# State-space and convolution stage on one core: operations grouped, elementwise work moved from GpSimd to VectorE

## The chip, the cores and the metric

One core of a Trainium2 chip runs one inference step of a hybrid decoder layer as a single program. The metric is the device time of one execution in microseconds (us). Five engines work side by side: TensorE (PE; its weight loads are listed as PEld), VectorE (DVE), ScalarE (ACT), GpSimd (POOL) and SyncE (SP), which here issues the transfers.

## The reference, cut to what matters

A prompt of 1024 tokens and 8 samples of 4 tokens go through the same layer. First comes the mixer, which the change touches: a convolution group and a state-space group side by side. Then follow cross-attention into 256 memory tokens and a SwiGLU network, each with a norm before and after.

```python
def token_mixer(h, conv_buf, ssm_h0, ...):
    z = h @ w_in
    a, g, u = z[..., :512], z[..., 512:1024], z[..., 1024:]
    v = a * jax.nn.sigmoid(g)
    v_ext = jnp.concatenate([conv_buf, v], axis=1)
    c = jax.nn.silu(layer_norm(causal_depthwise_conv(v_ext, w_dw, b_dw), ln_g, ln_b))
    s, h_last = s5_layer(u, ssm_h0, ...)
    return jnp.concatenate([c, s], axis=-1) @ w_out, conv_new, h_last

def s5_layer(u, h0, ...):              # 32 groups of 16 channels, 64 complex states each
    a_bar = jnp.exp(lam * dt)
    b_bar = ((a_bar - 1.0) / lam)[:, :, None] * b_mat
    bu = jnp.einsum("btgp,gnp->btgn", uf, b_bar)
    bu = bu.at[:, 0].add(a_bar * h0)
    _, hs = lax.associative_scan(_ssm_combine, (a_seq, bu), axis=1)
    y = jnp.einsum("btgn,gpn->btgp", hs, c_mat).real + d_skip * uf
    y = jax.nn.gelu(y)
    return y * jax.nn.sigmoid(y @ w_glu), hs[:, -1]
```

## The kernel before, in words

Activations lie with channels on the 128 partitions. The 1056 tokens are two blocks b of 2 x 264 columns: 8 sample columns and 256 prompt columns in each half. Matrix products use each operand as a high and a low part, three products each.

The program opens with `tokens_in`, which turns the token rows over on TensorE into tiles tagged `xf` (13 buffers, line 289), and with small tables for the state space: `turns`, `pw` (powers of a_bar), `pwr` (the same reversed), `rho`, `cmat` and `bbar`. Then `run(filler(), s5_stream())` (line 822) interleaves two streams, and this is the stage that the change touches.

`s5_stream` goes through 16 pairs of channel groups; two pairs make a super group `sg`. Four time steps are folded into one column, so each pair scans 256 columns. `s5_matrices` (line 682) builds the block matrices `ebd` (from `bbar` and `pwr`, four steps) and `fbd` (from `cmat` and `pw`, five steps): complex products, written as two real products into `ct0` and `ct1` and a sum or difference per output part `o` and per half `g` of the partitions. `s5_matrices2` transposes `ebd` (psS), multiplies it with `fbd` (psK, with the skip term `dd`) and copies both out. `s5_table` (line 669) makes cosine and sine of the turn of each column for one pair: the sum of a coarse and a fine turn and the subtraction of the rounded turn on GpSimd, the rounding on VectorE, absolute value and two sines on ScalarE, into a table `tab` of two buffers. `s5_states` (line 735) multiplies the inputs on TensorE into a PSUM tile, copies the sample columns out on ScalarE (`wsam`), turns the rest back (X and Y on VectorE, their sums on GpSimd), scans real and imaginary part with `tensor_tensor_scan` (M, VectorE), turns forward again (X on VectorE, Y on GpSimd) and writes `hx` (VectorE); GpSimd writes the start values into `hx` and the final state into `hfin`. `s5_outputs` (line 766) makes the outputs of the pair two behind on TensorE and ScalarE's gelu. X, Y and M have two buffers each, `hx` three. psS, psK and the output tile `py` share two PSUM tiles.

`filler` carries the convolution group in four blocks `ct` of 128 channels. `conv_input` (line 560) projects gate and value, with the sigmoid on ScalarE and the gate's second multiplication (`sg`, line 577) on GpSimd. `conv` (line 622) makes the prompt's convolution as products with small banded matrices `cm`, built in turn by VectorE and GpSimd in two buffers (line 639), five products into `pcv` each. `conv_samples` (line 610) convolves the samples' columns: for each of 8 samples a product with the taps on GpSimd into `sp` (one buffer) and two reductions on VectorE, put behind all else by a low priority. `conv_tail` packs the new convolution state (`pk`) on GpSimd.

The order on each engine is fixed when the program is built: a scheduler places instructions by priority (order in the source, moved by `high_priority`) against a simulated time line, and a tile is handed out when a buffer of its tag is free. On the chip each engine works through its own list in order and waits by semaphores.

Of the kernel before, what the change touches and what calls it, by code (L numbers as in the profile page):

```python
# [8 lines left out]
F32 = mybir.dt.float32  # L9
# [3 lines left out]
AF = mybir.ActivationFunctionType  # L13
# [5 lines left out]
P = 128  # L19
# [23 lines left out]
def decode_step(ctx: ExitStack, tc: tile.TileContext, I, O):  # L43
# [36 lines left out]
    def tt(out, a, b, op, eng=None):  # L80
        (eng or dve).tensor_tensor(out, a, b, op)  # L81
# [198 lines left out]
    def tokens_in(b):  # L280
        for k in range(KT):
            c = slice(k * P, (k + 1) * P)
            pt = mm_tile(f"xt{b}{k}")
            for s in range(2):
                q = slice(32 * (2 * b + s), 32 * (2 * b + s) + 8)
                for i in range(2):
                    pe.transpose(pt[:, s, 8 + i * P:8 + (i + 1) * P], rows[b][s][i][:, c], ident)
                pe.transpose(pt[:, s, 0:8], srows[q, c], ident[q, q])
            xt = startp.tile([P, 2, W], F32, tag="xf", bufs=13, name=f"xf{b}{k}")
            act.activation(xt, pt[:, :, :W], AF.Copy)  # L290
            sync.dma_start(xres[b][k], xt)
# [219 lines left out]
    pe.transpose(ph[:, 128:256], h0row[:, 1, :], ident)  # L511
    h0 = sp5.tile([P, 2, NB, 16], F32, tag="h0", name="h0")
    dve.tensor_copy(h0, ph[:, 0:256].rearrange("p (i b a) -> p i b a", i=2, b=NB))
    cmat = sp5.tile([P, 2, 16, 16], F32, tag="cmat", name="cmat")
    for i, sign in enumerate((1.0, -1.0)):
        pc = sm_tile(f"pc{i}")
        for j in range(4):
            pe.transpose(pc[:, j * P:(j + 1) * P], crow[i][:, j, :], ident)
        pcv = pc.rearrange("p (a g q) -> p a g q", g=2, q=16)
        for g in range(2):  # L520
            q = slice(64 * g, 64 * g + 64)
            act.activation(cmat[q, i], pcv[q, :, g, :], AF.Copy, scale=sign)

    bbar = sp5.tile([P, 2, 16, 16], F32, tag="bbar", name="bbar")
    b1 = unit("b1", F32, (P, 16, 16), "co")

    def bc(x, n):
        return x.unsqueeze(2).to_broadcast([P, x.shape[1], n])

    for o, (x, y, op) in enumerate(((f_re, f_im, ALU.subtract), (f_im, f_re, ALU.add))):  # L530
        tt(bbar[:, o], bc(x, 16), bmat[:, 0], ALU.mult, pool)
        tt(b1, bc(y, 16), bmat[:, 1], ALU.mult, pool)
        tt(bbar[:, o], bbar[:, o], b1, op, pool)

    run(gt[1])
    with tc.high_priority(offset=1000000):
# [23 lines left out]
    def conv_input(ct):  # L560
# [10 lines left out]
        for b in range(2):  # L571
            pg = mm_tile(f"pg{ct}{b}")
            dense(pg, wgh, wgl, h[b])
            sg = tmp(f"sg{ct}{b}")
            tt(sg, pg[:, :, :W], r0[b], ALU.mult)
            act.activation(sg, sg, AF.Sigmoid)
            tt(sg, sg, r0[b], ALU.mult, pool)
            yield
            pa = mm_tile(f"pa{ct}{b}")
            dense(pa, wah, wal, h[b])  # L580
            tt(view(vt, 2 * b * CH + 4, [(CH, 2), (4 * CH, 2), (1, P)]), view(pa, 8, [(512, 2), (1, 2), (2, P)]),
               view(sg, 8, [(W, 2), (1, 2), (2, P)]), ALU.mult)
# [6 lines left out]
    def conv_tail(ct):  # L589
# [7 lines left out]
                           pst[:, 128 * i:128 * i + 120].rearrange("p (b r) -> p b r", r=30), AF.Copy)  # L597
        background(conv_samples, ct)
        pk = mx.tile([P, 64], F32, tag="pk", name=f"pk{ct}")
        pool.tensor_copy(pk[:, 0:32].rearrange("p (s b) -> p s b", s=4), vs[:, :, 30:34].rearrange("p b s -> p s b"))  # L600
        pool.tensor_copy(pk[:, 32:64].rearrange("p (j s) -> p s j", s=8), vt[:, :, CH - 4:])
        pr = mm_tile(f"pcr{ct}")[:, 0]
        pe.transpose(pr[:64, 0:P], pk, ident)
        cr = mx.tile([64, P], F32, tag="cr", name=f"cr{ct}")
# [5 lines left out]
    def conv_samples(ct):  # L610
        vs = vss[ct]
        w = taps[:, ct]
        for i in range(8):
            sp = mx.tile([P, 4, TAPS], F32, tag="sp", bufs=1, name=f"sp{ct}{i}")
            tt(sp, view(vs, 34 * i, [(1, 4), (1, TAPS)]), w.unsqueeze(1).to_broadcast([P, 4, TAPS]), ALU.mult, pool)
            for b in range(2):
                dve.tensor_reduce(co[b][ct][:, :, i:i + 1], sp[:, 2 * b:2 * b + 2, :].unsqueeze(2), AX.X, ALU.add)
        for b in range(2):
            o = co[b][ct][:, :, 0:8]
            dve.tensor_scalar(o, o, par[:, 16 + ct:17 + ct], None, op0=ALU.add)  # L620

    def conv(ct):
# [10 lines left out]
        for q in range(2):  # L633
            pc = pcv[:, q]
            ob = mx.tile([P, 4, P], F32, tag="ob", bufs=2, name=f"ob{ct}{q}")
            for g4 in range(4):
                g, gg = 4 * q + g4, 8 * ct + 4 * q + g4
                cm = mx.tile([P, 5, 16, 8], F32, tag="cm", bufs=2, name=f"cm{gg}")
                tt(cm, wsh[:, g].rearrange("p (d t) -> p d t", t=8).unsqueeze(2).to_broadcast([P, 5, 16, 8]),
                   cmask.unsqueeze(1).unsqueeze(3).to_broadcast([P, 5, 16, 8]), ALU.mult, pool if g % 2 else dve)  # L640
                o = pc[:, g4 * P:(g4 + 1) * P]
                for d in range(5):
                    pe.matmul(o, lhsT=cm[:, d].rearrange("p c t -> p (c t)"), rhs=vf[:, g, 4 - d:CH - d],  # L643
# [24 lines left out]

    def s5_table(pair):

        f1, f2 = (mx.tile([P, 256], F32, tag=f"turn{i}", name=f"turn{i}_{pair}") for i in range(2))
        tab = s5t(f"tab{pair}", "tab")
        tt(f1.rearrange("p (i j) -> p i j", i=16), turns[:, 0, pair].unsqueeze(2).to_broadcast([P, 16, 16]),
           turns[:, 1, pair].unsqueeze(1).to_broadcast([P, 16, 16]), ALU.add, pool)
        dve.tensor_scalar(f2, f1, MAGIC, MAGIC, op0=ALU.add, op1=ALU.subtract)
        tt(f1, f1, f2, ALU.subtract, pool)
        act.activation(f2, f1, AF.Abs)
        act.activation(tab[:, 1], f1, AF.Sin, scale=6.283185)
        act.activation(tab[:, 0], f2, AF.Sin, scale=-6.283185, bias=half_pi)
        S5["tab", pair] = tab  # L680

    def s5_matrices(sg):
        p0 = 2 * sg
        pr = slice(p0, p0 + 2)
        eb, fb = ebd[0], fbd[sg % 2]
        for (mat, n, dst, src, ops, eng) in ((bbar, 4, eb, pwr, (ALU.subtract, ALU.add), dve),
                                             (cmat, 5, fb, pw, (ALU.add, ALU.subtract), dve)):
            def pwb(i):
                return src[:, i, :, pr].rearrange("p s a -> p a s").unsqueeze(3).to_broadcast([P, 2, n, 16])

            def mb(i):
                return mat[:, i, pr, :].unsqueeze(2).to_broadcast([P, 2, n, 16])

            for o in range(2):
                t = [mx.tile([P, 2, 5, 16], F32, tag=f"ct{i}", name=f"ct{i}_{sg}{n}{o}")[:, :, :n] for i in range(2)]
                tt(t[0], pwb(0), mb(o), ALU.mult, eng)
                tt(t[1], pwb(1), mb(1 - o), ALU.mult, eng)
                for g in range(2):
                    q = slice(64 * g, 64 * g + 64)
                    tt(dst[q, :, o, :, g, :], t[0][q], t[1][q], ops[o], eng)  # L700
        S5["mat", sg] = (eb, fb)

    def s5_matrices2(sg):
# [7 lines left out]
        act.activation(sm, psS.rearrange("p (a i m) -> p a i m", a=2, i=2), AF.Copy)  # L711
        psK = sm_tile(f"psK{sg}")
        dd = mx.tile([32, 2, 32], F32, tag="dd", name=f"dd{sg}")
        tt(dd, ident[:32, None, :32].to_broadcast([32, 2, 32]), dT[:, pr].unsqueeze(2).to_broadcast([32, 2, 32]), ALU.mult, pool)
        for a in range(2):
            o = psK[:32, a * P:(a + 1) * P]
            for i in range(2):
# [17 lines left out]
    def s5_states(pair):  # L735
# [10 lines left out]
        X, Y = s5t(f"X{pair}", "X"), s5t(f"Y{pair}", "Y")  # L746
        tt(X, pw_[:, :, 8:W], cb, ALU.mult)
        tt(Y, pw_[:, :, 8:W], sb, ALU.mult)
        tt(X[:, 0], X[:, 0], Y[:, 1], ALU.add, pool)
        tt(X[:, 1], X[:, 1], Y[:, 0], ALU.subtract, pool)  # L750
        M = s5t(f"M{pair}", "M")
        for i in range(2):
            dve.tensor_tensor_scan(out=M[:, i], data0=rho[:, pair:pair + 1].to_broadcast([P, 256]), data1=X[:, i],  # L753
                                   initial=0.0, op0=ALU.mult, op1=ALU.add)
        tt(X, M, cb, ALU.mult)
        tt(Y, M, sb, ALU.mult, pool)
        hx = s5t(f"hx{pair}", "hx", F32, (P, 2, W))
# [23 lines left out]
    def s5_stream():  # L781
# [786 lines left out]
```

## Time and profile before

| | before |
|---|---|
| runs shown, us | 1632.19, 1634.96, 1637.48 (median 1634.96) |
| profiled execution, us | 1629.99, its span 1628.3 |
| busy over the span, us | PE 1501.8, PEld 1454.1, DVE 1004.9, ACT 685.6, POOL 327.6 |
| mean granted TensorE clock | 0.972 |
| DMA | 194.33 MB, mean 119 GB/s |

Busy times come from one profiled execution; the span is the time from its first to its last instruction. Shares over the whole span are averages over stages with different limits. PEclk is the share of full TensorE clock that was granted in a stretch. A releaser is the work whose end let a waiting instruction go. A line such as L81 is a helper's (every `tensor_tensor` stands there), so groups are told apart by the names of what they write and read.

### The profile page before, as it was taken

Reading aid. Unit: us, or ns where it says so; the run is one execution under the profiler, and the core shown is the slowest. Engines: PE = TensorE matmul, PEld = TensorE weight load, DVE = VectorE, ACT = ScalarE, POOL = GpSimd, SP = SyncE. Lnnn points to the kernel's source line nnn. Section 1 sums busy time; section 2 is a strip of 40 time slices with the busy share of each in tenths; the row PEclk is TensorE's granted clock in tenths of the full one; section 3 lists DMA queues with packets and bytes.
Section 4 is the critical chain, followed back from the end, with each engine's and each line's share of the span. In section 5 each row is a group of like instructions: output and inputs, shape, how many; then the busy total and the mean of one; then the engine's idle time right before and its main releaser. Section 6 shows DMA issues by size and latency. Waiting matters only on the chain. (4 is left out here: it accounts for less than half of the span.)

```text
span 1628.3 us, 29327 instructions
## 1 busy us (share of the span) xinstructions
PE 1501.8 (92%) x11731; PEld 1454.1 (89%) x11731; DVE 1004.9 (62%) x1689; ACT 685.6 (42%) x1242; POOL 327.6 (20%) x409
## 2 busy tenths in 40 slices
PE   7999889889999979878968899999999999999995
PEld 5888878889999979778968899999999999999995
DVE  6889786466468855484486877666555542444345
ACT  6444534457564544374355643333333334122122
POOL 1366566330334420051120000000000000000005
PEclk9998999999999989989989999999999999999998
DMA  8522223456244503454436643333222234232124
GB/s 232 166 73 70 65 71 101 139 155 202 78 138 152 184 14 117 143 168 140 142 118 182 218 141 124 124 119 99 80 79 79 67 113 149 89 101 69 50 66 158
DMA packets 216116, 194.33 MB, mean 119 GB/s; under 512 B 21900, under 2 KB 180036, under 8 KB 215972
## 3 DMA queue, kind: packets, MB, share of 16 engines
q1 hardware_dynamic: 215852, 192.30, 38.3%
q8 instruction: 92, 1.51, 0.4%
q14 instruction: 44, 0.36, 0.1%
q10 hardware_dynamic: 128, 0.16, 0.0%
HBM read 146.33 MB, written 46.51 MB: 118 GB/s over the span
## 5 line engine op out<-in xcount | busy, mean ns | idle before, releaser
L1497 POOL COPY ysam<-ya 128x8 f32<-128x8 f32 x32 | 5.6, 192 | 745.9 <-DVE ya L81 745.1
L81 DVE TENSOR_TENSOR ya<-ya,fd 128x528 f32<-128x528 f32 x64 | 45.1, 704 | 105.8 <-PE fd L191 105.8
L176 ACT ACTIVATE hi_wd<-st_wd 128x1024 fp32r<-128x1024 f32 x20 | 21.2, 1060 | 121.5 <-PE fd L191 121.3
L191 PE MATMUL pao<-oth,hi_wa 128*128 128x264 f32 x256 | 53.8, 292 | 14.4 <-ACT mg L979 13.3
L81 DVE TENSOR_TENSOR c<-c,X 128x528 f32<-128x528 f32 x51 | 35.9, 703 | 39.7 <-PE X L1310 39.7
L191 PEld LDWEIGHTS pao<-oth,hi_wa 128*128 128x128 f32 x256 | 40.9, 194 | 15.2 <-ACT mg L979 13.9
L191 PE MATMUL pao<-otl,hi_wa 128*128 128x264 f32 x256 | 53.7, 291 | 0.0
L191 PE MATMUL pao<-oth,lo_wa 128*128 128x264 f32 x256 | 53.2, 289 | 0.5 <-DVE lo_wa L84 0.5
L643 PE MATMUL pcv<-vf,cm 128*128 128x128 f32 x320 | 45.2, 292 | 7.2 <-ACT ob L645 4.5
L643 PEld LDWEIGHTS pcv<-vf,cm 128*128 128x128 f32 x320 | 41.9, 206 | 9.0 <-issue 5.7
L191 PEld LDWEIGHTS pao<-oth,lo_wa 128*128 128x128 f32 x256 | 40.8, 193 | 0.8 <-DVE lo_wa L84 0.7
L191 PEld LDWEIGHTS pao<-otl,hi_wa 128*128 128x128 f32 x256 | 41.0, 194 | 0.1
L84 DVE TENSOR_TENSOR lo_wa<-st_wa,hi_wa 128x1024 fp32r<-128x1024 f32 x16 | 19.4, 1214 | 34.0 <-ACT hi_wa L176 34.0
L84 DVE TENSOR_TENSOR kl<-pkr,kh 128x512 fp32r<-128x512 f32 x32 | 21.9, 690 | 28.7 <-ACT kh L89 28.5
L84 DVE TENSOR_TENSOR lo_wd<-st_wd,hi_wd 128x1024 fp32r<-128x1024 f32 x20 | 24.5, 1225 | 24.4 <-ACT hi_wd L176 21.2
L224 DVE RECIPROCAL r_n<-r_n 128x528 f32<-128x528 f32 x8 | 27.6, 3450 | 12.0 <-ACT r_n L223 12.0
L753 DVE TENSOR_TENSOR_SCAN M<-rho,X 128x256 f32<-128x256 f32 x32 | 29.8, 956 | 7.4 <-POOL X L81 7.3
L89 ACT ACTIVATE wc<-t 128x512 fp32r<-128x512 f32 x22 | 13.9, 632 | 47.2 <-PE X L1310 25.1
L89 ACT ACTIVATE kh<-pkr 128x512 fp32r<-128x512 f32 x32 | 18.9, 598 | 30.7 <-PE pkr L1135 29.5
L81 DVE TENSOR_TENSOR c<-c,c 128x528 f32<-128x528 f32 x45 | 31.6, 702 | 0.1
L645 ACT ACTIVATE ob<-pcv,cbias 128x128 f32<-128x128 f32 x32 | 11.6, 364 | 46.4 <-PE pcv L643 46.3
L1385 ACT ACTIVATE c<-Z 128x528 f32<-128x528 f32 x22 | 13.5, 612 | 41.4 <-PE Z L1310 41.4
(2047 smaller groups left out, 5720.1 us busy)
## 6 DMA issues: line engine op xcount, KB each, us to landing
hr<-hid SPq DMA_DIRECT2D x44, 264.0 KB
ww<-in_w_gate_dram SPq DMA_DIRECT2D x22, 512.0 KB
ww<-in_w_up_dram SPq DMA_DIRECT2D x22, 512.0 KB
st_wd<-in_w_down_dram SPq DMA_DIRECT2D x20, 512.0 KB
hid<-c SPq DMA_DIRECT2D x38, 264.0 KB
xo<-x SPq DMA_DIRECT2D x32, 264.0 KB
kr<-in_cache_mem_k_dram SPq DMA_DIRECT2D x32, 256.0 KB
st_wo<-in_w_out_dram SPq DMA_DIRECT2D x16, 512.0 KB
```

Source lines behind the costliest of these rows:

```text
L81: (eng or dve).tensor_tensor(out, a, b, op)
L84: eng.tensor_tensor(lo, x, hi.bitcast(F32), ALU.subtract)
L89: act.activation(hi, x, AF.Copy)
L176: act.activation(hi[:, :cols], stv, AF.Copy)
L191: pe.matmul(out, lhsT=a, rhs=part(b), start=first and i == 0, stop=last and i == 2)
L224: dve.reciprocal(r, r)
L643: pe.matmul(o, lhsT=cm[:, d].rearrange("p c t -> p (c t)"), rhs=vf[:, g, 4 - d:CH - d], start=d == 0, stop=d == 4)
L645: act.activation(ob[:, g4], o, AF.Identity, bias=cbias[:, gg:gg + 1])
L753: dve.tensor_tensor_scan(out=M[:, i], data0=rho[:, pair:pair + 1].to_broadcast([P, 256]), data1=X[:, i], initial=0.0, op0=ALU.mult, op1=AL ...
L1385: act.activation(c22, Z[:, :, :W], AF.Copy)
L1497: pool.tensor_copy(ysam[:, n, 2 * b + s, :], yacc[b][n][:, s, 0:8])
```

## The change

In `s5_matrices` the two real products of a complex one are made for both output parts at once: `cmat` and `bbar` get a second copy of themselves with parts swapped and signed (written by ScalarE in the opening), and the products go into tiles of the tags Y and M. `s5_table` works on two pairs at a time, in VectorE instead of GpSimd, its rounded turns in a tile of tag Y; a table buffer holds two pairs. X, Y and M have one buffer each. In `s5_states` all sums and products are on VectorE; ScalarE writes the start values and the final state, which is now an extra column of `hx`. The gate's second multiplication, all `cm` and `dd` are on VectorE, the packing of `pk` is on ScalarE. `conv_samples` makes one product and one reduction for all samples of a block, in a tile of tag Y. `xf` has 12 buffers. GpSimd keeps `bbar`'s three operations per part, memory fills and what follows the stage.

```diff
-            xt = startp.tile([P, 2, W], F32, tag="xf", bufs=13, name=f"xf{b}{k}")
+            xt = startp.tile([P, 2, W], F32, tag="xf", bufs=12, name=f"xf{b}{k}")
...
-            act.activation(cmat[q, i], pcv[q, :, g, :], AF.Copy, scale=sign)
+            act.activation(cmat[q, 0, :, i], pcv[q, :, g, :], AF.Copy, scale=sign)
+            act.activation(cmat[q, 1, :, 1 - i], pcv[q, :, g, :], AF.Copy, scale=-1.0)
...
-        tt(bbar[:, o], bc(x, 16), bmat[:, 0], ALU.mult, pool)
+        re_ = bbar[:, 0, :, o]
+        tt(re_, bc(x, 16), bmat[:, 0], ALU.mult, pool)
...
+        act.activation(bbar[:, 1, :, 1 - o], re_, AF.Copy, scale=-1.0 if o else 1.0)
...
-    SBUFS = {"X": 2, "Y": 2, "M": 2, "hx": 3, "uf": 2, "sm": 2, "tab": 2}
+    SBUFS = {"X": 1, "Y": 1, "M": 1, "hx": 3, "uf": 2, "sm": 2, "tab": 2}
...
-            tt(sg, sg, r0[b], ALU.mult, pool)
+            tt(sg, sg, r0[b], ALU.mult)
...
-        pool.tensor_copy(pk[:, 0:32].rearrange("p (s b) -> p s b", s=4), vs[:, :, 30:34].rearrange("p b s -> p s b"))
-        pool.tensor_copy(pk[:, 32:64].rearrange("p (j s) -> p s j", s=8), vt[:, :, CH - 4:])
+        act.activation(pk[:, 0:32].rearrange("p (s b) -> p s b", s=4), vs[:, :, 30:34].rearrange("p b s -> p s b"), AF.Copy)
+        act.activation(pk[:, 32:64].rearrange("p (j s) -> p s j", s=8), vt[:, :, CH - 4:], AF.Copy)
...
-        for i in range(8):
-            sp = mx.tile([P, 4, TAPS], F32, tag="sp", bufs=1, name=f"sp{ct}{i}")
-            tt(sp, view(vs, 34 * i, [(1, 4), (1, TAPS)]), w.unsqueeze(1).to_broadcast([P, 4, TAPS]), ALU.mult, pool)
-            for b in range(2):
-                dve.tensor_reduce(co[b][ct][:, :, i:i + 1], sp[:, 2 * b:2 * b + 2, :].unsqueeze(2), AX.X, ALU.add)
+        wb = w.unsqueeze(1).unsqueeze(1).to_broadcast([P, NB, 2, TAPS])
         for b in range(2):
+            sp = s5t(f"sp{ct}{b}", "Y", F32, (P, NB, 2, TAPS))
+            tt(sp, view(vs, 2 * b, [(34, NB), (1, 2), (1, TAPS)]), wb, ALU.mult)
+            dve.tensor_reduce(view(co[b][ct], 0, [(1, NB), (W, 2)]), sp, AX.X, ALU.add)
...
-                   cmask.unsqueeze(1).unsqueeze(3).to_broadcast([P, 5, 16, 8]), ALU.mult, pool if g % 2 else dve)
+                   cmask.unsqueeze(1).unsqueeze(3).to_broadcast([P, 5, 16, 8]), ALU.mult)
...
-        f1, f2 = (mx.tile([P, 256], F32, tag=f"turn{i}", name=f"turn{i}_{pair}") for i in range(2))
-        tab = s5t(f"tab{pair}", "tab")
-        tt(f1.rearrange("p (i j) -> p i j", i=16), turns[:, 0, pair].unsqueeze(2).to_broadcast([P, 16, 16]),
-           turns[:, 1, pair].unsqueeze(1).to_broadcast([P, 16, 16]), ALU.add, pool)
+        f1, f2 = mx.tile([P, 2, 256], F32, tag="turn0", name=f"turn0_{pair}"), s5t(f"turn1_{pair}", "Y")
+        tab = s5t(f"tab{pair}", "tab", F32, (P, 2, 2, 256))
+        two = slice(pair, pair + 2)
+        tt(f1.rearrange("p a (i j) -> p a i j", i=16), turns[:, 0, two].unsqueeze(3).to_broadcast([P, 2, 16, 16]),
+           turns[:, 1, two].unsqueeze(2).to_broadcast([P, 2, 16, 16]), ALU.add)
         dve.tensor_scalar(f2, f1, MAGIC, MAGIC, op0=ALU.add, op1=ALU.subtract)
-        tt(f1, f1, f2, ALU.subtract, pool)
-        act.activation(f2, f1, AF.Abs)
+        tt(f1, f1, f2, ALU.subtract)
+        act.activation(tab[:, 0], f1, AF.Abs)
         act.activation(tab[:, 1], f1, AF.Sin, scale=6.283185)
-        act.activation(tab[:, 0], f2, AF.Sin, scale=-6.283185, bias=half_pi)
+        act.activation(tab[:, 0], tab[:, 0], AF.Sin, scale=-6.283185, bias=half_pi)
...
-            for o in range(2):
-                t = [mx.tile([P, 2, 5, 16], F32, tag=f"ct{i}", name=f"ct{i}_{sg}{n}{o}")[:, :, :n] for i in range(2)]
-                tt(t[0], pwb(0), mb(o), ALU.mult, eng)
-                tt(t[1], pwb(1), mb(1 - o), ALU.mult, eng)
+        for mat, n, dst, src in ((bbar, 4, eb, pwr), (cmat, 5, fb, pw)):
+            t = [s5t(f"ct{i}_{sg}{n}", "YM"[i], F32, (P, 2, n, 2, 16)) for i in range(2)]
+            for i in range(2):
+                tt(t[i].rearrange("p a s o q -> p a s (o q)"),
+                   src[:, i, :, pr].rearrange("p s a -> p a s").unsqueeze(3).to_broadcast([P, 2, n, 32]),
+                   mat[:, i, pr].rearrange("p a o q -> p a (o q)").unsqueeze(2).to_broadcast([P, 2, n, 32]), ALU.mult)
+            for a in range(2):
                 for g in range(2):
                     q = slice(64 * g, 64 * g + 64)
-                    tt(dst[q, :, o, :, g, :], t[0][q], t[1][q], ops[o], eng)
+                    tt(dst[q, a, :, :, g, :], t[0][q, a].rearrange("p s o q -> p o s q"),
+                       t[1][q, a].rearrange("p s o q -> p o s q"), ALU.add)
...
-        tt(X[:, 0], X[:, 0], Y[:, 1], ALU.add, pool)
-        tt(X[:, 1], X[:, 1], Y[:, 0], ALU.subtract, pool)
+        tt(X[:, 0], X[:, 0], Y[:, 1], ALU.add)
+        tt(X[:, 1], X[:, 1], Y[:, 0], ALU.subtract)
...
-        tt(Y, M, sb, ALU.mult, pool)
-        hx = s5t(f"hx{pair}", "hx", F32, (P, 2, W))
-        pool.tensor_copy(hx[:, :, 0:8], h0[:, :, :, pair])
+        tt(Y, M, sb, ALU.mult)
+        hx = s5t(f"hx{pair}", "hx", F32, (P, 2, W + 1))
+        act.activation(hx[:, :, 0:8], h0[:, :, :, pair], AF.Copy)
...
-        tt(hfin[:, 0, pair:pair + 1], X[:, 0, 255:], Y[:, 1, 255:], ALU.subtract, pool)
-        tt(hfin[:, 1, pair:pair + 1], X[:, 1, 255:], Y[:, 0, 255:], ALU.add, pool)
+        act.activation(hfin[:, :, pair:pair + 1], hx[:, :, W:], AF.Copy)
...
-            if p < 15:
+            if p % 2 and p < 15:
                 s5_table(p + 1)
```

## Rows read from the trace of the kernel before

**Rows 1.** Busy us and, in brackets, instructions of each engine by stretch.
```profile
core 0: us, PE busy (x) PEld busy (x) DVE busy (x) ACT busy (x) POOL busy (x), PEclk, DMA share, GB/s
60.00:290.00 230.00, 204.51 (x1429) 187.64 (x1427) 178.55 (x352) 97.65 (x196) 138.21 (x204) 0.93 0.27 77
290.00:335.00 45.00, 38.92 (x295) 37.11 (x294) 23.79 (x47) 21.43 (x44) 18.52 (x20) 0.92 0.46 140
...
700.00:1628.00 928.00, 875.87 (x7063) 865.51 (x7061) 527.39 (x791) 336.24 (x600) 62.84 (x76) 0.98 0.37 116
```

**Rows 2.** Waits, 60 to 290 us: who for whom, total us, times, longest.
```profile
ACT L678 <- DVE X L81: 33.9, 10, 5.6
...
ACT turn L677 <- POOL turn L81: 24.0, 10, 4.0
...
PE psK L718 <- ACT yg L776: 12.2, 3, 4.6
POOL dd L81 <- PE psK L720: 11.2, 3, 5.8
POOL sg L81 <- ACT sg L576: 11.1, 6, 5.1
...
DVE co L617 <- POOL sp L81: 8.5, 11, 1.7
...
DVE hx L81 <- POOL Y L81: 7.8, 9, 1.2
POOL cm L81 <- PE pcv L643: 7.8, 1, 7.8
...
DVE turn L675 <- POOL turn L81: 2.7, 4, 0.8
```

**Rows 3.** Timeline of ACT and PE, 212 to 220 us: start, duration, instruction, idle before.
```profile
215.28 0.42 ACT L678 ACTIVATE tab<-turn 128x256 f32<-128x256 f32 x1 [1.82 <-POOL Y L81]
...
219.81 0.42 PE L718 MATMUL psK<-fbd,ebd 128*32 128x128 f32 x1 [4.65 <-ACT yg L776]
```

**Rows 4.** Groups on DVE, 60 to 290 us: busy us, mean ns, idle before.
```profile
L753 DVE TENSOR_TENSOR_SCAN M<-rho,X 128x256 f32<-128x256 f32 x32 | 29.8, 956 | 7.4 <-POOL X L81 7.3
L81 DVE TENSOR_TENSOR ct<-pw,cmat 128x160 f32<-128x160 f32 x32 | 15.7, 532 | 0.2
L81 DVE TENSOR_TENSOR X<-M,tab 128x512 f32<-128x512 f32 x16 | 15.6, 978 | 0.3
L81 DVE TENSOR_TENSOR fbd<-ct,ct 64x160 f32<-64x160 f32 x32 | 14.6, 455 | 0.7
...
L81 DVE TENSOR_TENSOR X<-pw,tab 128x512 f32<-128x512 f32 x16 | 11.0, 686 | 9.8 <-ACT wsam L743 9.7
```

**Rows 5.** Tiles, 60 to 335 us: ns shortest/median/longest, first and last start.
```profile
L753 DVE TENSOR_TENSOR_SCAN M<-rho,X x32: 659/926/1707, 81.4 to 265.8; 128x256 f32<-128x256 f32 x32
L81 DVE TENSOR_TENSOR X<-M,tab x16: 691/693/1771, 83.2 to 266.8; 128x512 f32<-128x512 f32 x16
...
L81 DVE TENSOR_TENSOR ct<-pw,cmat x32: 300/324/1453, 63.7 to 240.7; 128x160 f32<-128x160 f32 x32
L81 DVE TENSOR_TENSOR fbd<-ct,ct x32: 289/322/1309, 64.9 to 243.0; 64x160 f32<-64x160 f32 x32
...
L81 DVE TENSOR_TENSOR hx<-X,Y x32: 407/419/1505, 85.1 to 269.4; 128x255 f32<-128x255 f32 x32
...
L81 DVE TENSOR_TENSOR cm<-wsh,cmask x16: 794/824/1905, 59.7 to 321.4; 128x640 f32<-128x640 f32 x16
...
L81 DVE TENSOR_TENSOR sg<-pg,r_x x8: 691/702/708, 77.3 to 291.8; 128x528 f32<-128x528 f32 x8
...
L675 DVE TENSOR_SCALAR turn<-turn x16: 283/294/840, 63.5 to 238.2; 128x256 f32<-128x256 f32 x16
...
L617 DVE TENSOR_REDUCE co<-sp x64: 186/209/221, 129.2 to 323.8; 128x2 f32<-128x62 f32 x64
```

**Rows 6.** Timeline of ACT, 41 to 42 us.
```profile
41.41 0.62 ACT L290 ACTIVATE xf<-xt 128x528 f32<-128x528 f32 x1 [4.09 <-PE xt L288]
```

More of the change, by code (lines that the diff above doesn't have):

```diff
@@ L513, in decode_step @@
     dve.tensor_copy(h0, ph[:, 0:256].rearrange("p (i b a) -> p i b a", i=2, b=NB))
-    cmat = sp5.tile([P, 2, 16, 16], F32, tag="cmat", name="cmat")
+    cmat = sp5.tile([P, 2, 16, 2, 16], F32, tag="cmat", name="cmat")
     for i, sign in enumerate((1.0, -1.0)):
@@ L521, in decode_step @@
             q = slice(64 * g, 64 * g + 64)
-            act.activation(cmat[q, i], pcv[q, :, g, :], AF.Copy, scale=sign)
-    bbar = sp5.tile([P, 2, 16, 16], F32, tag="bbar", name="bbar")
+            act.activation(cmat[q, 0, :, i], pcv[q, :, g, :], AF.Copy, scale=sign)
+            act.activation(cmat[q, 1, :, 1 - i], pcv[q, :, g, :], AF.Copy, scale=-1.0)
+    bbar = sp5.tile([P, 2, 16, 2, 16], F32, tag="bbar", name="bbar")
     b1 = unit("b1", F32, (P, 16, 16), "co")
@@ L530, in decode_step @@
     for o, (x, y, op) in enumerate(((f_re, f_im, ALU.subtract), (f_im, f_re, ALU.add))):
-        tt(bbar[:, o], bc(x, 16), bmat[:, 0], ALU.mult, pool)
+        re_ = bbar[:, 0, :, o]
+        tt(re_, bc(x, 16), bmat[:, 0], ALU.mult, pool)
         tt(b1, bc(y, 16), bmat[:, 1], ALU.mult, pool)
-        tt(bbar[:, o], bbar[:, o], b1, op, pool)
+        tt(re_, re_, b1, op, pool)
+        act.activation(bbar[:, 1, :, 1 - o], re_, AF.Copy, scale=-1.0 if o else 1.0)
     run(gt[1])
@@ L669, in s5_table @@
     def s5_table(pair):
-        f1, f2 = (mx.tile([P, 256], F32, tag=f"turn{i}", name=f"turn{i}_{pair}") for i in range(2))
-        tab = s5t(f"tab{pair}", "tab")
-        tt(f1.rearrange("p (i j) -> p i j", i=16), turns[:, 0, pair].unsqueeze(2).to_broadcast([P, 16, 16]),
-           turns[:, 1, pair].unsqueeze(1).to_broadcast([P, 16, 16]), ALU.add, pool)
+        f1, f2 = mx.tile([P, 2, 256], F32, tag="turn0", name=f"turn0_{pair}"), s5t(f"turn1_{pair}", "Y")
[3 more added lines that the diff above has]
+           turns[:, 1, two].unsqueeze(2).to_broadcast([P, 2, 16, 16]), ALU.add)
         dve.tensor_scalar(f2, f1, MAGIC, MAGIC, op0=ALU.add, op1=ALU.subtract)
-        tt(f1, f1, f2, ALU.subtract, pool)
-        act.activation(f2, f1, AF.Abs)
+        tt(f1, f1, f2, ALU.subtract)
+        act.activation(tab[:, 0], f1, AF.Abs)
         act.activation(tab[:, 1], f1, AF.Sin, scale=6.283185)
-        act.activation(tab[:, 0], f2, AF.Sin, scale=-6.283185, bias=half_pi)
-        S5["tab", pair] = tab
+        act.activation(tab[:, 0], tab[:, 0], AF.Sin, scale=-6.283185, bias=half_pi)
+        for a in range(2):
+            S5["tab", pair + a] = tab[:, :, a]
     def s5_matrices(sg):
@@ L685, in s5_matrices @@
         eb, fb = ebd[0], fbd[sg % 2]
[L686 to L692, printed above, removed]
-            for o in range(2):
-                t = [mx.tile([P, 2, 5, 16], F32, tag=f"ct{i}", name=f"ct{i}_{sg}{n}{o}")[:, :, :n] for i in range(2)]
-                tt(t[0], pwb(0), mb(o), ALU.mult, eng)
-                tt(t[1], pwb(1), mb(1 - o), ALU.mult, eng)
+        for mat, n, dst, src in ((bbar, 4, eb, pwr), (cmat, 5, fb, pw)):
[4 more added lines that the diff above has]
+                   mat[:, i, pr].rearrange("p a o q -> p a (o q)").unsqueeze(2).to_broadcast([P, 2, n, 32]), ALU.mult)
+            for a in range(2):
                 for g in range(2):
                     q = slice(64 * g, 64 * g + 64)
-                    tt(dst[q, :, o, :, g, :], t[0][q], t[1][q], ops[o], eng)
+                    tt(dst[q, a, :, :, g, :], t[0][q, a].rearrange("p s o q -> p o s q"),
+                       t[1][q, a].rearrange("p s o q -> p o s q"), ALU.add)
         S5["mat", sg] = (eb, fb)
@@ L713, in s5_matrices2 @@
         dd = mx.tile([32, 2, 32], F32, tag="dd", name=f"dd{sg}")
-        tt(dd, ident[:32, None, :32].to_broadcast([32, 2, 32]), dT[:, pr].unsqueeze(2).to_broadcast([32, 2, 32]), ALU.mult, pool)
+        tt(dd, ident[:32, None, :32].to_broadcast([32, 2, 32]), dT[:, pr].unsqueeze(2).to_broadcast([32, 2, 32]), ALU.mult)
         for a in range(2):
@@ L755, in s5_states @@
         tt(X, M, cb, ALU.mult)
-        tt(Y, M, sb, ALU.mult, pool)
-        hx = s5t(f"hx{pair}", "hx", F32, (P, 2, W))
-        pool.tensor_copy(hx[:, :, 0:8], h0[:, :, :, pair])
+        tt(Y, M, sb, ALU.mult)
+        hx = s5t(f"hx{pair}", "hx", F32, (P, 2, W + 1))
+        act.activation(hx[:, :, 0:8], h0[:, :, :, pair], AF.Copy)
         pool.memset(hx[:, :, 8:9], 0.0)
-        tt(hx[:, 0, 9:], X[:, 0, 0:255], Y[:, 1, 0:255], ALU.subtract)
-        tt(hx[:, 1, 9:], X[:, 1, 0:255], Y[:, 0, 0:255], ALU.add)
-        tt(hfin[:, 0, pair:pair + 1], X[:, 0, 255:], Y[:, 1, 255:], ALU.subtract, pool)
-        tt(hfin[:, 1, pair:pair + 1], X[:, 1, 255:], Y[:, 0, 255:], ALU.add, pool)
+        tt(hx[:, 0, 9:], X[:, 0], Y[:, 1], ALU.subtract)
+        tt(hx[:, 1, 9:], X[:, 1], Y[:, 0], ALU.add)
+        act.activation(hfin[:, :, pair:pair + 1], hx[:, :, W:], AF.Copy)
         S5["h", pair] = hx
@@ L773, in s5_outputs @@
         for i in range(2):
-            pe.matmul(o, lhsT=fb[:, a, i, 1:5].rearrange("p t g q -> p (t g q)"), rhs=hx[:, i], start=False, stop=i == 1)
+            pe.matmul(o, lhsT=fb[:, a, i, 1:5].rearrange("p t g q -> p (t g q)"), rhs=hx[:, i, :W], start=False, stop=i == 1)
         yg = mx.tile([P, W], F32, tag="yg", bufs=2, name=f"yg{pair}")
```

## The prediction

> **What bounds the kernel now.** I read the time by stretches first. From 335 us on TensorE is busy 94% of the time (876 of 928 us in the long last stretch) at nearly the full granted clock, and nothing of the change lies there: that part I take as fixed [rows 1]. The state-space and convolution stage, 60 to 290 us, is different: TensorE 204.5 of 230 us at a mean granted clock of 0.93, VectorE 178.6, GpSimd 138.2. TensorE alone would need less: 0.93 is a mix of the two levels, 2.4 and 1.2 GHz, with 14% of the time at the lower one, so 16 us of its busy time are half-speed loss, and its work at full clock is 188 us. So neither engine fills the stage. What fills it is the waiting between them.
>
> The waits come next [rows 2]. VectorE's idle time is 230 - 178.6 = 51.4 us. Of it 8.5 + 7.8 + 2.7 us end with a GpSimd result (the tap products, Y, the turns), and before the scan 7.3 us more with its X: 26.3 us together; 9.7 us end with the ScalarE copy that reads the state product first [rows 2, 4]. TensorE's largest wait, 12.2 us in three stalls, is for a PSUM tile that the gelu of an earlier pair frees. That gelu is late because ScalarE works in order and stands still before the table sines: 33.9 us for VectorE to free a table buffer, 24.0 us for GpSimd's turns. One stall in order of time: the sine waits 1.82 us for GpSimd's Y, the gelu comes behind it, and TensorE restarts at 219.81 after 4.65 us [rows 3]. The chain to follow is therefore pair by pair: product, VectorE, GpSimd, VectorE, GpSimd, VectorE, outputs.
>
> **The price of an operation.** The means of the VectorE operations beside their shortest times show a second loss. X from M and the table, both in SBUF, takes 978 ns in the mean and 691 at best; the same size from PSUM takes 686 in the mean [rows 4, 5]. The scan takes 956 against 659, a product for the c matrices 532 against 300, its sum 455 against 289. Operations with one PSUM input are not slowed; those with two SBUF inputs are, while GpSimd runs. The excess is 32 x 0.297 + 16 x 0.287 + 32 x 0.232 + 32 x 0.166 = 9.5 + 4.6 + 7.4 + 5.3 = 26.8 us. The 58 sisters for the b matrices I put at the smallest of these, 0.166: 9.6 us. Together 36 us that VectorE loses beside GpSimd. The Trainium skill ("SBUF — State Buffer", Who interferes with whom) says a VectorE instruction with two SBUF inputs contends with a GpSimd one that reads SBUF, and one with a single SBUF input does not. The 978 against 686 ns agree; by that rule the excess vanishes whole once GpSimd only fills memory.
>
> **The change part by part, on VectorE** (shortest times, since no GpSimd read is left in the stage; all [rows 5]):
> - Y from M: 16 x 0.69 = 11.1 us. The two half-size sums into X: 32 x 0.41 (a 255-wide sum) = 13.1.
> - The tables: 8 calls of two 512-wide sums (0.69 each) and one 512-wide rounding. That rounding is not shown; it lies between 0.28 (256 wide) and 0.69, I take 0.45. 8 x 1.83 = 14.6, less the old 16 x 0.28 = 4.5: 10.1. Bounds 8.8 to 12.
> - The gate's second product, 8 x 0.70 = 5.6; the convolution matrices, 16 x 0.79 = 12.7; dd, eight small ones, 0.3 each at most (the smallest matrix sum is 64 x 160 at 0.29): 2.
> - The samples' convolution: 8 products and 8 reductions of 496 elements, up to 0.69 each, 11, for 64 small reductions of 0.209, 13.4: -2.
> - The matrices: 64 products become 32 of 256 or 320 elements, 0.41 and 0.48 on the line between 0.41 at 255 and 0.69 at 512: 14.3 for 64 at 0.30 = 19.2, so -5. Their 64 sums stay 64, of the same size.
> Sum 11.1 + 13.1 + 10.1 + 5.6 + 12.7 + 2 - 2 - 5 = 47.6 us. About a quarter of the gate and matrix terms (4.6) belongs to the last channel block, after 290 us, and lies there beside VectorE's 21 idle us of 45 [rows 1]. So +43, less 36 of contention: VectorE goes from 178.6 to about 185.6 us.
>
> **On ScalarE**: copies of hx (16), hfin (16), pk (8), cmat (4) and bbar (2), against 24 table operations fewer that each become twice as wide. A 256-wide table operation takes 0.42 us [rows 3], so 46 x 0.42 = 19 us is the upper bound and ScalarE would stand at 117 of 230: hidden by its own idle time. If that cover failed where a copy stands ahead of the state product's read, it would lengthen the 9.7 us wait by at most that.
> **Tables for two pairs at a time**: the two buffers now hold four pairs, so a sine waits for the pair before last, not the last; this should take most of the 33.9 us, and the 24.0 us behind GpSimd's turns. What is late next is VectorE itself.
> **Buffers**: X, Y and M go from two to one and are shared with the table, the matrices and the tap products. Every reader and writer of them is now VectorE, which is in order anyway: 0, and up to the 30 us below if the order comes out badly. One start buffer fewer: the thirteenth of them is filled at 41.4 us after waiting 4.09 us for TensorE, not for a buffer [rows 6]: 0, at worst a like wait. No DMA is added or moved past another.
> **Waits that VectorE takes over**: GpSimd waited 11.1 us for the sigmoid, 11.2 us for psK before dd and 7.8 us for the convolution's products before refilling cm [rows 2]. On an in-order VectorE such a wait holds back the scan chain queued behind it, and TensorE and the gelu wait for that. Bounds 0 and 30.1. VectorE has other work that can be put ahead, as before 290 us it hardly waited for TensorE; I take a tenth, 3 us.
>
> **The sum.** VectorE's stage is busy time plus what idle remains: 185.6 + (51.4 - 26.3) + 3 = 213.7 us for 230, a gain of 16.3. TensorE's 188 us fit in with 25 to spare where it had 42. The profiled execution took 1629.99 us, so 1613.7 for it; the runs shown have a median of 1634.96, 5 above, so I forecast 1634.96 - 16.3 = 1618.7 us.
>
> **Rivals.**
> 1. Better: with ScalarE no longer held, the 9.7 us behind its read go too, and nothing is inherited. VectorE then needs 185.6 + 51.4 - 26.3 - 9.7 = 201 us, 29 less: 1606. The floor is TensorE's 188, 42 less: 1593. Against it: two engines this full seldom meet so well.
> 2. Slower: VectorE inherits GpSimd's 30.1 us of waiting whole, in order: 185.6 + 25.1 + 30.1 = 240.8, so +11: 1646. It decides at 19 us inherited, two thirds of it. For it: single buffers of X, Y, M leave less to run instead. Against it: GpSimd waited so long because it had nothing else.
> 3. Also slower: the contention does not come back. VectorE is then 178.6 + 43 = 221.6, with 28.1 of idle 249.7: +20, 1655. Against it, 686 beside 978 ns [rows 4]. The Trainium skill ("Perfetto Trace Analysis", Optimizing Scalar/DVE Operations) says that when VectorE is saturated, moving work off it may make sense, even to GpSimd, but that the two share a read port so that moving between them might not help. Its first half speaks for this rival, its second half against; the traces bear the second.
> 4. No change: the gains on VectorE are taken back by the order of TensorE's queue, which stands behind psK as now, so that only the three stalls are moved: within 5 us of 1635.
>
> **Chances.** Forecast 0.52, rival 1 0.18, rival 2 0.14, rival 3 0.05, rival 4 0.11. About 0.3%, 5 us, is what can be told from no change. Faster 0.70, same 0.11, slower 0.19. The forecast's own range is 1609 to 1629 (3 us inherited becoming 0 to 8, the unshown prices, the moved order behind it). To hold 8 in 10 it reaches over rival 1 to TensorE's floor, and up to rival 2's value: 1594 to 1645.
>
> **What would show it.** Right: GpSimd below 20 us between 60 and 290; the scan near 0.67 us and X from M near 0.69 in the mean; VectorE idle for GpSimd gone; VectorE over 85% of a stage that ends some 16 us earlier; the sines no longer waiting for X; psK's wait for the gelu under 5 us; fewer stretches of TensorE at 1.2 GHz. Wrong: VectorE waiting over 20 us for the sigmoid, psK or pcv (rival 2); scan and X unchanged in the mean (rival 3); VectorE shorter and TensorE's stalls as long as now (rival 4).

## The result, and the profile after

The changed kernel takes 1607.34 us in the median (1601.02 to 1612.82, 4 runs) against 1635.4 for the kernel before: a ratio of 0.9834, 95% interval 0.9804 to 0.9863, or 28 us less. The forecast was 1618.7. The time moved the way that was forecast and lies inside the stated range of 1594 to 1645, but the forecast gain of 16 us was too small by 12, and the narrower range of 1609 to 1629, which stood for the forecast's own mechanism, was missed by 2 us. The profiled execution took 1601.02 us, its span is 1599.3.

The stretch that answers to [rows 1], and a pair that compares about equal work: from 60 us on, TensorE has made 1585 products by 317 us before and by 290 us after (their order differs, so they are not all the same ones). Columns: length, busy us and instructions of each engine, granted clock, DMA.

```profile
60.00:317.00 257.00, 226.01 (x1585) 207.73 (x1583) 192.23 (x380) 112.40 (x225) 147.96 (x216) 0.93 0.29 83
```

That was the kernel before; the kernel after:

```profile
60.00:290.00 230.00, 215.77 (x1585) 200.79 (x1585) 195.72 (x392) 107.21 (x229) 6.29 (x22) 0.98 0.33 92
...
700.00:1599.00 899.00, 851.74 (x6887) 842.98 (x6887) 504.31 (x761) 317.24 (x553) 48.21 (x61) 0.98 0.36 114
```

257 - 230 = 27 us: nearly the whole gain. On TensorE it is 31.0 - 14.2 = 16.8 us of idle time and 226.0 - 215.8 = 10.2 us of busy time, as the granted clock rose from 0.93 to 0.98 of 2.4 GHz. Before, seven pieces of this stretch ran at 1.2 GHz, 36 us in all, and each began in or just behind idle time of TensorE (at 117.1 us, for instance, behind a gap of 3.4 us that ended at 115.5); after, there are two, 10 us. On VectorE the busy time grew by only 3.5 us, and the idle time fell from 64.8 to 34.3. The long last stretch keeps its shape.

Groups on VectorE, 60 to 290 us, kernel after (busy, mean ns | idle before, releaser), against [rows 4]:

```profile
L81 DVE TENSOR_TENSOR cm<-wsh,cmask 128x640 f32<-128x640 f32 x28 | 23.2, 830 | 0.8 <-PE pcv L646 0.7
L754 DVE TENSOR_TENSOR_SCAN M<-rho,X 128x256 f32<-128x256 f32 x32 | 20.4, 674 | 0.0
...
L81 DVE TENSOR_TENSOR X<-X,Y 128x256 f32<-128x256 f32 x32 | 12.1, 420 | 0.4
...
L81 DVE TENSOR_TENSOR X<-M,tab 128x512 f32<-128x512 f32 x16 | 11.0, 689 | 0.4
L81 DVE TENSOR_TENSOR X<-pw,tab 128x512 f32<-128x512 f32 x16 | 11.0, 688 | 6.4 <-ACT wsam L744 6.2
...
L81 DVE TENSOR_TENSOR ct<-pw,cmat 128x320 f32<-128x320 f32 x16 | 7.1, 486 | 0.0
...
L679 DVE TENSOR_SCALAR turn<-turn 128x512 f32<-128x512 f32 x8 | 3.4, 425 | 0.2
```

X from M now costs what X from PSUM costs, 689 beside 688 ns, and the scan fell from 956 to 674. The waits of the same stretch, against [rows 2]:

```profile
ACT hfin L763 <- DVE hx L81: 23.7, 14, 4.3
...
DVE dd L81 <- PE psK L721: 8.0, 5, 2.5
DVE turn L81 <- ACT tab L682: 7.5, 7, 1.3
...
DVE X L81 <- ACT wsam L744: 6.2, 6, 1.3
...
DVE sg L81 <- ACT sg L580: 3.0, 5, 0.7
```

No wait of VectorE for GpSimd is left, and psK waits for the gelu no more. ScalarE's 33.9 us for table buffers are gone; ScalarE stands before hfin instead. VectorE has inherited dd and sg (11 us), and waits for ScalarE to free a turn tile (7.5), which nobody had named.

The last surprise is the order in which the two streams end. The outputs of the state space and the convolution's products, before and then after (shortest/median/longest ns, first and last start):

```profile
L774 PE MATMUL py<-hx,fbd x64: 383/386/647, 99.8 to 271.3; 128*128 128x264 f32 x64
...
L643 PE MATMUL pcv<-vf,cm x320: 270/275/582, 135.6 to 328.7; 128*128 128x128 f32 x160
```

```profile
L774 PE MATMUL py<-hx,fbd x64: 385/386/490, 102.2 to 281.0; 128*128 128x264 f32 x64
...
L646 PE MATMUL pcv<-vf,cm x320: 270/275/582, 122.2 to 303.8; 128*128 128x128 f32 x160
```

The chain of the pairs ends 10 us later than before. The convolution ends 25 us earlier, and with it the stage. In all the profiled runs of this document the span ends 1295 to 1306 us after the last of the convolution's products starts, whatever the pairs do.

### The profile page after: what moved, and what is told of

The parts are those of the page before. It is cut to its first block, busy times and chain, and to the rows that moved or that the text cites. A ratio compares the mean times of both kernels' runs of the same rounds, so it can differ in the third digit from the quotient of the medians.

```text
span 1599.3 us, 29061 instructions
## 1 busy us (share of the span) xinstructions
PE 1491.0 (93%) x11731; PEld 1446.4 (90%) x11731; DVE 1010.8 (63%) x1697; ACT 683.6 (43%) x1258; POOL 181.8 (11%) x209
## 5 line engine op out<-in xcount | busy, mean ns | idle before, releaser
L89 ACT ACTIVATE wc<-t 128x512 fp32r<-128x512 f32 x22 | 13.9, 632 | 47.3 <-PE X L1310 25.2
L84 DVE TENSOR_TENSOR lo_wo<-st_wo,hi_wo 128x1024 fp32r<-128x1024 f32 x16 | 19.9, 1245 | 17.5 <-ACT hi_wo L176 17.5
L81 DVE TENSOR_TENSOR t<-ww,t 128x512 f32<-128x512 f32 x44 | 30.2, 687 | 0.6
```

Of the source, the lines that this page charges most:

```text
L84: eng.tensor_tensor(lo, x, hi.bitcast(F32), ALU.subtract)
L89: act.activation(hi, x, AF.Copy)
```

## The experiments

The theories: A, the gain is GpSimd leaving the chain of each pair (its hops and its contention); B, ScalarE is no longer held by table buffers; C, fewer operations make room on VectorE; D, contention alone. E and F came up on the way. Ratios are to the kernel before on the same chip, with 95% intervals; 0.01 is 16 us.

**moves_only.** The kernel before, with the engines of the change and nothing else of it: the sums, Y, gate, cm, tables, dd and sp on VectorE, the copies of hx, hfin and pk on ScalarE.

```diff
-        tt(X[:, 0], X[:, 0], Y[:, 1], ALU.add, pool)
+        tt(X[:, 0], X[:, 0], Y[:, 1], ALU.add)
...
-        tt(Y, M, sb, ALU.mult, pool)
+        tt(Y, M, sb, ALU.mult)
...
```

> The kernel before with the engine moves alone: everything that the change takes from GpSimd goes to VectorE or ScalarE, but matrices, tables and samples stay in their small operations, tables are for one pair and X, Y, M keep two buffers. Theory A (the gain is GpSimd leaving the chain of each pair, its hops and its contention): most of the 28 us, 1608 to 1618 us. Rival B (the gain is ScalarE no longer held by table buffers, so the two-pair tables): little, 1625 to 1635, with ScalarE still waiting some 30 us before its sines. Rival C (fewer operations make room on VectorE): slower than 1625, because VectorE carries 144 small operations more than it needs.

1603.69 us, 0.9826 (0.9803 to 0.9849): the whole gain. B and C are not needed for it. ScalarE's 33.9 us before its sines became 5.1 without the two-pair tables. VectorE's busy time over the span is 1015.0 us, 4 more than in the kernel after, so the grouping is worth little there.

This run also settles which stream ends the stage (kernel moves_only):

```profile
L773 PE MATMUL py<-hx,fbd x64: 385/386/490, 98.7 to 244.1; 128*128 128x264 f32 x64
...
L643 PE MATMUL pcv<-vf,cm x320: 270/275/582, 127.5 to 299.8; 128*128 128x128 f32 x160
```

The pairs end 37 us sooner than in the kernel after, the convolution 4 us sooner, and the spans are 1599.4 and 1599.3 us. So the late end of the pairs in the kernel after is not the work of the moves, and the end of the pairs does not set the time.

**grouping_only.** The kernel after with every operation that had moved back on its old engine.

```diff
-        tt(Y, M, sb, ALU.mult)
+        tt(Y, M, sb, ALU.mult, pool)
...
```

> The kernel after with every elementwise operation of the stage back on the engine it had before; the grouping (matrices, two-pair tables, samples) and the single X, Y, M buffers stay. Theory A: little of the gain or a loss, 1630 to 1645, with VectorE again waiting 20 us or more for GpSimd. Rival B: most of the gain, 1607 to 1615. Rival C: about half, 1618 to 1625.

1623.6 us, 0.9953 (0.9937 to 0.9968): 8 us, between A and C (the time itself lies in C's range, but the kernel before took 1632.15 us on this chip, and 8 us are less than half of the gain). VectorE waits for GpSimd as before, and the scan is as slow as before (kernel grouping_only, VectorE, 60 to 290 us):

```profile
L754 DVE TENSOR_TENSOR_SCAN M<-rho,X 128x256 f32<-128x256 f32 x32 | 31.6, 1024 | 17.0 <-POOL X L81 17.0
```

So 28 us for the moves and 8 for the grouping, but 27 together: beside the moves, the grouping adds nothing. Grouping means here the package with single buffers of X, Y and M, whose own price comes below; what grouping alone adds to the moves was not measured.

**idle_pool** and **idle_half.** The kernel after with 14 or 7 products per pair on GpSimd that nobody waits for.

```diff
         S5["h", pair] = hx
+        for i in range(14):
+            idle = tiny.tile([P, P], F32, tag="rd", bufs=3, name=f"idle{pair}{i}")
+            tt(idle, ones, wsam[:, 0, pair, 0:1].to_broadcast([P, P]), ALU.mult, pool)
```

> The kernel after with 14 products of 128x128 per pair on GpSimd that read two SBUF tiles and that nobody waits for, some 100 us of GpSimd in all, about as much as the change took away. It tells contention from hops. If the contention is what mattered (rival D): VectorE's busy time rises by 25 to 40 us and 15 us or more of the 28 are lost, 1622 to 1632. Theory A with the hops as the larger part: the scan's mean rises from 0.67 to 0.8 us or more, but the time stays under 1618.

> The kernel after with 7 instead of 14 unneeded products per pair on GpSimd, some 50 us of them. idle_pool gave 1627 us, 20 above the kernel after. If contention costs VectorE in proportion (rival D): half of it, 1614 to 1620, with VectorE's busy time up by some 10 us. If there is a threshold instead: within 4 us of 1607 or of 1627.

1627.27 us, 0.9967 (0.9951 to 0.9983), and 1615.83 us, 0.9906 (0.9874 to 0.9938). The engine busy times of the whole span, of the kernels after, idle_half and idle_pool:

```profile
PE 1491.0 (93%) x11731; PEld 1446.4 (90%) x11731; DVE 1010.8 (63%) x1697; ACT 683.6 (43%) x1258; POOL 181.8 (11%) x209
```
```profile
PE 1498.7 (93%) x11731; PEld 1453.0 (90%) x11731; DVE 1018.9 (63%) x1697; ACT 683.0 (42%) x1258; POOL 238.0 (15%) x321
```
```profile
PE 1504.9 (93%) x11731; PEld 1459.0 (90%) x11731; DVE 1031.0 (63%) x1697; ACT 683.3 (42%) x1258; POOL 311.2 (19%) x433
```

VectorE does the same 1697 instructions. In the three traces those of VectorE and of TensorE stand in the same order through the stage, and between 60 and 290 us no engine waits for the added products, so contention is what is left to explain the difference. Of VectorE's groups, 60 to 290 us, the scan (kernel idle_pool):

```profile
L754 DVE TENSOR_TENSOR_SCAN M<-rho,X 128x256 f32<-128x256 f32 x30 | 24.2, 842 | 0.0
```

It goes from 674 to 842 ns in the mean; X from PSUM, 688 ns in the kernel after, takes 685. With 56 us more of GpSimd VectorE is busy 8.1 us longer, with 129 us 20.2 us, which is less than the 25 to 40 expected. The time grows by 12 and 22 us by the ratios (8 and 20 by the medians), and the convolution's last product starts 10 and 21 us later. Useless work on another engine undoes most of the change, so contention alone can account for some 20 of the 28 us (D holds), and a us that it takes from VectorE in this stage costs the kernel about a us, give or take several us in all. Part of it comes by way of TensorE: its busy time grows by 7.7 and 13.9 us at a lower granted clock (0.973 and 0.970 over the span, after 0.980).

**chain_pool.** The kernel after with only the two sums into X and the product Y of each pair on GpSimd.

```diff
-        tt(X[:, 0], X[:, 0], Y[:, 1], ALU.add)
-        tt(X[:, 1], X[:, 1], Y[:, 0], ALU.subtract)
+        tt(X[:, 0], X[:, 0], Y[:, 1], ALU.add, pool)
+        tt(X[:, 1], X[:, 1], Y[:, 0], ALU.subtract, pool)
...
-        tt(Y, M, sb, ALU.mult)
+        tt(Y, M, sb, ALU.mult, pool)
```

> The kernel after with only the two sums into X and the product Y of each pair back on GpSimd, some 51 us of GpSimd work as in idle_half (1616 us), but here VectorE waits for it, and VectorE carries 24 us less. If contention alone counts (rival D): as idle_half less the work taken from VectorE, 1600 to 1614. If the hops between VectorE and GpSimd inside a pair count as much (theory A): slower than idle_half in spite of the lighter VectorE, 1617 to 1630.

1622.48 us, 0.9941 (0.9918 to 0.9964). The stretch 60 to 290 us of chain_pool, then of idle_half:

```profile
60.00:290.00 230.00, 211.79 (x1532) 197.38 (x1531) 176.99 (x324) 98.41 (x208) 55.51 (x66) 0.97 0.28 78
```
```profile
60.00:290.00 230.00, 211.85 (x1543) 197.55 (x1542) 193.43 (x374) 100.98 (x217) 58.27 (x128) 0.97 0.29 81
```

GpSimd is busy about as long in both. In chain_pool VectorE is busy 16 us less, and TensorE is no further for it (1532 products beside 1543): VectorE waits 6.2 us for X, 5.7 for Y and 3.5 for the start column of `hx`, which GpSimd fills behind them: 15.4 together, about as much as its work shrank. So waiting for GpSimd uses up what the lighter VectorE saves. The intervals of the two runs overlap and TensorE's order is not the same in them, so the size is not settled; that a lighter VectorE brought nothing is.

**tables_single.** The kernel after with turn tiles and tables for one pair; the rounded turns still have tag Y.

```diff
-            if p % 2 and p < 15:
+            if p < 15:
                 s5_table(p + 1)
...
```

> The kernel after with the tables made for one pair at a time (two buffers of one pair), still on VectorE. Rival B: ScalarE waits 30 us or more for table buffers again and 10 to 20 us of the gain are lost, 1617 to 1627. Theory A: within 5 us of the kernel after, 1603 to 1613; eight more small sums cost VectorE some 3 us.

1625.92 us, 0.9955 (0.9938 to 0.9972). As large a loss as B foretold, but not by B's way: ScalarE's wait for table buffers did not return. VectorE waits for the turn tile, which a sine still reads (kernel tables_single, VectorE, 60 to 290 us):

```profile
L81 DVE TENSOR_TENSOR turn<-turns 128x256 f32<-128x256 f32 x16 | 6.8, 423 | 14.6 <-ACT tab L681 14.5
```

That is 7 us more than in the kernel after, of 19 lost. moves_only has tables for one pair too and waits 1.0 us there.

**tables_single_two_buffers**, **moves_single_buffers** and **grouped_two_buffers** vary the buffers.

The first starts from tables_single, the second from moves_only, the third from the first.

```diff
-    SBUFS = {"X": 1, "Y": 1, "M": 1, "hx": 3, "uf": 2, "sm": 2, "tab": 2}
+    SBUFS = {"X": 2, "Y": 2, "M": 1, "hx": 3, "uf": 2, "sm": 2, "tab": 2}
```
```diff
-    SBUFS = {"X": 2, "Y": 2, "M": 2, "hx": 3, "uf": 2, "sm": 2, "tab": 2}
+    SBUFS = {"X": 1, "Y": 1, "M": 1, "hx": 3, "uf": 2, "sm": 2, "tab": 2}
```
```diff
-        f1, f2 = mx.tile([P, 256], F32, tag="turn0", name=f"turn0_{pair}"), s5t(f"turn1_{pair}", "Y", F32, (P, 256))
+        f1, f2 = (mx.tile([P, 256], F32, tag=f"turn{i}", name=f"turn{i}_{pair}") for i in range(2))
```

> tables_single, which lost 19 us of the gain, with two buffers for X and Y again (the room comes from the smaller tables); the table's rounded turns still share Y's tag. If the loss came from the table taking the only Y between every two pairs (theory E): it comes back, 1600 to 1610. If it came from ScalarE and the one-pair tables themselves (rival B): 1620 to 1628 as in tables_single.

> moves_only (1604 us) with one buffer each for X, Y and M; tables, matrices and samples keep tiles of their own. Since VectorE alone reads and writes the three, theory A of the prediction says 0: 1600 to 1609. Theory E (single buffers cost because the next pair cannot start while VectorE waits): 1612 to 1625.

> A version meant to beat both: engine moves and grouped matrices and samples as in the kernel after, tables for one pair with turn tiles of their own as in the kernel before, X and Y with two buffers, M with one. It carries some 15 us less VectorE work than moves_only (1604). If VectorE's work is still the bound: 1590 to 1600. If the bound is now elsewhere (TensorE, order): 1600 to 1608. If single-pair tables cost by themselves: above 1612.

1614.2 us, 0.9897 (0.9866 to 0.9927): 9 to 12 of the 19 us come back with the second buffers (by the ratios, by the medians), so E, that single buffers of X and Y cost, holds for about half; the 1600 to 1610 that E foretold were missed. 1612.11 us, 0.9883 (0.9852 to 0.9914): single buffers cost moves_only some 8 us, although one engine alone uses them. Its interval only just parts from that of moves_only, so the size is loose. 1614.37 us, 0.9899 (0.9863 to 0.9935): the version meant to be best was not; a turn tile of its own changed nothing. Its time lies where one-pair tables that cost by themselves were expected, but moves_only has such tables and takes 1604. VectorE still waits 9.8 us there for the other turn tile and 8.9 for ScalarE's copy; whether the matrices and samples that share the tags of the pair hold it up is not shown.

**small_copies_pool** and **moves_small_copies_pool.** The copies of hx, hfin and pk on GpSimd instead of ScalarE, in the kernel after and in moves_only.

```diff
-        act.activation(hfin[:, :, pair:pair + 1], hx[:, :, W:], AF.Copy)
+        pool.tensor_copy(hfin[:, :, pair:pair + 1], hx[:, :, W:])
...
```

> The kernel after with only the small copies (hx start values, hfin, pk) back on GpSimd, which has nothing else to do; each reads 2 to 32 elements. In the kernel after ScalarE stands 23.7 us before hfin, waiting for hx. If that held back ScalarE's later work (theory F): 1597 to 1603. If it stood in time that nobody needed: 1604 to 1611.

> moves_only (1604 us) with the same small copies on GpSimd. Theory F: 1595 to 1601, the fastest of all; ScalarE waited only 9.2 us before hfin there. Otherwise 1601 to 1608.

1606.48 us, 0.985 (0.9832 to 0.9869), and 1604.15 us, 0.9835 (0.9808 to 0.9862): no change. F, that ScalarE's queue is held there, falls. ScalarE's 23.7 us before hfin stood in time that nobody needed.

**moves_samples_by_two.** moves_only with two samples per operation.

```diff
-        for i in range(8):
-            sp = mx.tile([P, 4, TAPS], F32, tag="sp", bufs=1, name=f"sp{ct}{i}")
+        for i in range(4):
+            sp = mx.tile([P, 2, 4, TAPS], F32, tag="sp", bufs=1, name=f"sp{ct}{i}")
```

> moves_only (1604 us) with the samples' convolution in operations for two samples at a time: 16 products and 32 reductions for 32 and 64, some 7 us less VectorE work, and nothing shared. If VectorE's work is still what bounds the stage: 1596 to 1601. If the work that is saved lay in time that nobody needed (the samples have the lowest priority): 1601 to 1607, as moves_only.

1605.96 us, 0.9837 (0.9813 to 0.9861): as moves_only. The samples' products and reductions took 14.2 us instead of 20.1, and the time did not fall. They have the lowest priority; not every us of VectorE is a us of the kernel. No version tried beats both kernels clearly; moves_only and the kernel after cannot be told apart.

## Why the prediction was right, point by point

**What bounds the stage.** Right that waits between engines fill it, and that VectorE is what is late next: idle_pool and idle_half show that what VectorE loses to contention the kernel loses. Wrong in one sentence: "The chain to follow is therefore pair by pair". That chain ends 10 us later and the stage 27 us earlier, and in moves_only it ends at 244 instead of 281 us at the same time of the kernel. The convolution, whose matrices need VectorE too, ends the stage.

**The prices.** Right within 6%: sums of 256 at 420 ns (0.41 taken), the 512-wide rounding at 425 (0.45), products of 320 at 486 (0.48), cm at 830 (0.79). Contention went as computed, the scan from 956 to 674 and X from M from 978 to 689 ns. The Trainium skill ("SBUF — State Buffer", Who interferes with whom) has GpSimd's reads contend with VectorE instructions of two SBUF inputs, and says that one with at most one such input, outside VectorE's 2-port modes, does not contend. In the kernel after that rule leaves next to nothing to contend, and X from M costs what X from PSUM costs; idle_pool, which puts such reads back, brings the scan to 842 ns and leaves X from PSUM at 685. The prediction left the exception out, and the rounding with its one SBUF input had been slowed too: 378 ns in the mean before, 283 at best.

**Busy time.** Forecast +7.0 us for VectorE up to 290 us, and with the last block's share 47.6 - 36 = +11.6; over the span it is 1010.8 - 1004.9 = +5.9, on the stretch of equal work +3.5. So this term was too dear by some 4 to 6 us. Contention that the 36 us leave out is of that size: `hx` fell from 491 to 421 ns (32 of them), the cm that VectorE had built already from 987 to 830 (16), the splits of weights `lo_wi` from 1335 to 1219 (10), 6 us together.

**The mis-sized term is "what idle remains".** The prediction took GpSimd's 26.3 us away, added 3 and kept the rest: 23.3 us less idle. On the stretch of equal work idle time fell by 64.8 - 34.3 = 30.5, which with the cheaper busy time gives the 27 us. Two errors lie in it. The stage was cut off at 290 us and the last convolution block put at nothing; but of the 64.8 us, 13.3 lay between 290 and 317, most of them VectorE's wait for the convolution's products before it refills cm (kernel before, 290 to 317 us):

```profile
DVE cm L81 <- PE pcv L643: 11.5, 3, 7.2
```

In the kernel after that wait is 0.7 us up to 290 and 0.6 behind it: 28 of the 32 matrices are built by then, where before VectorE had 6 of its 16 still to build. And the inherited waits came to some 12 us and not 3 (dd 8.0, sg 3.0, cm 0.7), with 7.5 for the turn tile on top: rival 2's mechanism was there, at a good third of its 30.1. The two errors work against each other, and the other waits that were kept in the sum shrank by some 11 us in small pieces, the one for ScalarE's read from 9.7 to 6.2 among them; so that the sum came out within 12 us is in part luck.

**Buffers at nothing** was wrong. That one engine alone reads and writes X, Y and M does not make a second buffer worthless: moves_single_buffers lost about 8 us, tables_single_two_buffers won 9 to 12. The cause in detail is open: from 87 us on VectorE's instructions stand in another order in moves_single_buffers than in moves_only, and whether it is that order or the waits of VectorE that nothing could fill was not separated.

**Tables.** "this should take most of the 33.9 us" came true, but moves_only shows that the two-pair tables need not be the reason. Why they pay in the kernel after (tables_single takes 19 us more) is open: second buffers of X and Y gave back about half of that, a turn tile of its own nothing more.

**The rivals.** 1 (better, 1606) is what happened in size, but not by its mechanism: of the 9.7 us behind ScalarE's read 6.2 stayed, and some 12 us were inherited where it had none. 2 was present in part. 3 fell with the scan's 674 ns; the Trainium skill's caution ("Perfetto Trace Analysis", Optimizing Scalar/DVE Operations) that moving work between VectorE and GpSimd might not help because they share a read port is borne out for work given to GpSimd: in idle_pool 129 us of it cost VectorE 20 us. 4 fell with psK's wait.

## What to carry to other kernels

Price an engine's help by what it takes from its neighbour: here a GpSimd operation that nobody waits for cost VectorE about 15% of its own length, and that came out as time because VectorE was the late engine. Work of VectorE that stood behind all else (moves_samples_by_two) did not. When work moves, split the change into moves alone and grouping alone before crediting either; here the moves alone brought the whole gain. Compare stretches of equal work (the same number of matrix products), not of equal time, or idle time at the stretch's end goes uncounted.

## What the runs showed that was not expected

A buffer that a single in-order engine writes and reads still had a price of some 8 us when it was alone. When the chain of the pairs ended said nothing about the time: at 244 us in moves_only and at 281 in the kernel after, at equal spans. And the engine waits that grew most, ScalarE's 23.7 us before hfin, were worth nothing when taken away.
